# MLP second layer: half of the low weights of 11 chunks made by negation on ScalarE and an adding transfer instead of a subtraction on VectorE

## The chip, the cores and the metric

The kernel runs on one core of a Trainium2 chip. The metric is the device time of one execution in microseconds; lower is better. The kernel before takes 2065.62 us (median of two runs, 2065.62 and 2065.63).

## The reference, cut to what matters

One layer of an encoder over 256 tokens of width 2048, all float32: a mixer of two branches (retention and gated DeltaNet), cross-attention into 256 memory tokens, and an MLP, each behind an RMSNorm and with a residual sum; a last RMSNorm. The change touches the MLP's second matrix only:

```python
h = rms_norm(x, norm_ffn_g[l])
x = x + jnp.square(jax.nn.relu(h @ w_ff1[l])) @ w_ff2[l]   # w_ff1: 2048 x 8192, w_ff2: 8192 x 2048
return rms_norm(x, norm_final_g)
```

## The kernel before, in words

All large products run on TensorE in a type of reduced precision (float32r). To keep float32 accuracy each operand is split into a high and a low half: high = the value rounded to that type, low = value - high. A product is then three matmuls, high x high, high x low, low x high, summed in PSUM (lines 134 to 136 in `products`).

Weights stream from HBM. `fetch` (L75) takes one quarter of a chunk: 512 rows x 512 columns, 1 MB, loaded by one DMA on SP's queue into `raw` (3 buffers), seen as four row blocks of 128. For each of two halves (i = 0, 1; two row blocks, 128 x 1024 elements, 512 KB) ScalarE writes the high half `whi` (L93) and VectorE the low half `wlo` by subtracting `whi` from `raw` (L94). `whi` and `wlo` have 4 buffers each, so two quarters are held. A `raw` buffer is free once the last of its two subtractions is done. All this has a high priority, so it is put as early as buffers allow.

`chunk` (L120) multiplies 256 tokens by 512 columns of a weight matrix: four quarters q, each with 4 row blocks x 2 token blocks x 3 matmuls = 24 matmuls of 512 columns, 12 per half. The MLP is done in four groups (`fb`, L1066), each over 2048 hidden features: first eight `blocks` of w_ff1 (L158, the other form of product, lines 172 and 174), then three chunks (n = 1, 2, 3, L1093) of w_ff2. Columns 0 to 511 of w_ff2 are done another way, by Strassen's seven products (`seven_products`, L1014), one call per 512 hidden features; each call loads one `raw` of 1 MB and makes two halves of 21 matmuls of 256 columns (L1041 to L1043). In the first three groups two of the four calls fall among the w_ff1 blocks and two among the chunks.

The order on each engine is set by a scheduler from priorities and its own estimates when the program is built; then every engine works through its list in order and waits on semaphores. SP issues all the weight loads. POOL has only a few small operations: it computes reciprocal roots (L222, L608).

The last chunk of the program (fb = 3, n = 3) takes its weights for quarters 2 and 3 into other buffers (`hold`).

Of the kernel before, what the change touches and what calls it, by code (L numbers as in the profile page):

```python
# [10 lines left out]
F32 = mybir.dt.float32  # L11
F32R = mybir.dt.float32r
I32 = mybir.dt.int32
AF = mybir.ActivationFunctionType
ALU = mybir.AluOpType
# [35 lines left out]
def trunk(ctx: ExitStack, tc: tile.TileContext, x, mem, positions, norm_mix_g, w_in, conv_w, gdn_a_log, gdn_dt_bias,  # L51
# [4 lines left out]
    act, vec, pool, pe = nc.scalar, nc.vector, nc.gpsimd, nc.tensor  # L56
# [15 lines left out]
        return psp.tile([P, 512], F32, name="b", tag="b", bufs=4)  # L72


    def fetch(pieces, k, n, rush=False, hold=None, at=0):  # L75

        raw = wp.tile([P, k * n], F32, name="raw", tag="raw", bufs=3)
        rv = raw.rearrange("p (k n) -> p k n", k=k)
        with tc.high_priority(offset=100000):
            for off, ap in pieces:  # L80
                src = ap.rearrange("(k p) n -> p k n", p=P)
                for ks in ((slice(0, k // 2), slice(k // 2, k)) if rush else (slice(0, k),)):
                    nc.sync.dma_start(rv[:, ks, off:off + ap.shape[1]], src[:, ks, :])
            got = []
            for i in range(2):
                if hold:
                    both = hold().both
                    hi, lo = (both[:, a:a + 2, :].rearrange("p a s -> p (a s)") for a in (0, 2))
                else:
                    hi, lo = (wp.tile([P, 1024 + ROOM], F32R, name=e, tag=e, bufs=4)[:, at:at + k * n // 2]  # L90
                              for e in ("whi", "wlo"))
                src = raw[:, i * k * n // 2:(i + 1) * k * n // 2]
                act.activation(hi, src, AF.Copy)  # L93
                vec.tensor_sub(lo, src, hi.bitcast(F32))  # L94
                got.append((hi.rearrange("p (k n) -> p k n", n=n), lo.rearrange("p (k n) -> p k n", n=n)))
        return got

# [19 lines left out]
    def quad_a():  # L117
        return new_quad(hqp, 5)

    def chunk(quads, pieces_of, evac, before=None, hold=None, between=None):  # L120


        ps = stream_ps()
# [5 lines left out]
        def products(q, i, part, halves):  # L129
            t, c0, c1, o = part  # L130
            xh, xl = (a[:, i, t * P:(t + 1) * P] for a in quads[q])
            wh, wl = (a[:, i % 2, c0:c1] for a in halves[i // 2])
            first, last = q == 0 and i == 0, q == 3 and i == 3
            pe.matmul(o, xh, wh, start=first, stop=False)  # L134
            pe.matmul(o, xh, wl, start=False, stop=False)  # L135
            pe.matmul(o, xl, wh, start=False, stop=last)  # L136

        for q in range(4):
            if q not in held:
                if before:  # L140
                    before(q)
                halves = fetch(pieces_of(q), 4, 512, rush=before is not None and q == 0)
                for i in range(4):
                    for part in parts:
                        products(q, i, part, halves)
                    if between and i % 2:
                        between()
# [7 lines left out]
    def cols(w, c0, n=512):  # L155
        return lambda q: [(0, w[q * 512:(q + 1) * 512, c0:c0 + n])]
# [178 lines left out]
    for k2 in range(8):  # L335
# [10 lines left out]
        for f in range(2):  # L346
            k = 2 * k2 + f
# [203 lines left out]
    for q in range(4):  # L551
        at = slice(32 * q, 32 * q + 32)
# [513 lines left out]
    for fb in range(4):  # L1066
# [6 lines left out]
        for b2 in range(8):  # L1073
# [3 lines left out]
            at = slice(b2 % 2 * 2, b2 % 2 * 2 + 2)  # L1077
# [15 lines left out]
        for n in range(1, 4):  # L1093
# [13 lines left out]
            def evac_last(t, ps, c0, c1):  # L1107
# [20 lines left out]
                for c in (0, 3, 1, 2):  # L1128
# [14 lines left out]
            last = fb == 3 and n == 3  # L1143
            sums = []
            chunk(hid, cols(w_ff2[0, fb * D:(fb + 1) * D, :], n * 512), evac_last if last else evac_o,
                  hold=quad_b if last else None)
            if n < 3 and fb < 3:
                strassen(n + 1)
            if fb == 3 and n == 1:
# [34 lines left out]
```

## Time and profile before

| | before |
|---|---|
| median of the runs | 2065.62 us |
| the profiled execution | 2066.05 us |
| its span (first to last instruction) | 2064.3 us |
| granted TensorE clock | 0.999 |
| moved by DMA | 408.28 MB, mean 198 GB/s |
| L94, low halves on VectorE | 668 of 1223 ns |
| L93, high halves on ScalarE | 668 of 1060 ns |
| the 11 chunks and their Strassen calls | four stretches; the first about 1465 to 1536 us |

The profile shows one execution. A busy engine is one with an instruction running; matmuls overlap, so one of 390 ns starts every 0.227 us. A row of the order of time gives start, duration, engine, line and tile; brackets give the idle time of the engine before it and what ended it. A DMA row on SP is its issue; its landing is listed apart.

### The profile page before, as it was taken

The page shows a single profiled execution, that of the slowest core. Times are in us where ns is not written, and L with a number is a line of the kernel's source. Part 1 is how long each engine was busy: PE and PEld are TensorE (multiplying, and loading weights), DVE is VectorE, ACT ScalarE, POOL GpSimd, SP SyncE. Part 2 cuts the span into 40 slices and gives each one's busy share as a digit, 9 for nine tenths or more (in the row PEclk, how much of TensorE's full clock was granted, in tenths as well). Part 3 has the DMA queues.
Part 4 walks back from the last instruction along what each step waited for, and adds up shares of the span by engine and source line. Part 5 has one row for each costly group of instructions (what it writes and reads, how often), then busy time and mean ns, then how long its engine had stood idle before and what let it go on. Part 6 is the DMA issues. An engine that isn't in the chain of part 4 may idle for free.

```text
span 2064.3 us, 29089 instructions
## 1 busy us (share of the span) xinstructions
PE 2045.1 (99%) x11240; PEld 1774.0 (86%) x11240; DVE 1510.3 (73%) x2381; ACT 1132.2 (55%) x1669; POOL 26.9 (1%) x37
## 2 busy tenths in 40 slices
PE   8999999999999999999999999999999999999998
PEld 6888888888888888888888898888888888988887
DVE  6785888588957896688767665768758756775885
ACT  7564664556445644565456555555546545554664
POOL 0000000000000000000000000000000000000000
PEclk9999999999999999999999999999999999999999
DMA  8797655465556555655567664565656566656653
GB/s 302 229 313 233 207 192 199 164 208 181 198 183 199 183 195 189 189 182 180 189 192 234 194 193 147 182 189 181 224 184 198 179 204 194 194 194 195 192 198 129
DMA packets 328313, 408.28 MB, mean 198 GB/s; under 512 B 31200, under 2 KB 236528, under 8 KB 328048
## 3 DMA queue, kind: packets, MB, share of 16 engines
q1 hardware_dynamic: 328032, 405.92, 61.0%
q8 instruction: 88, 1.44, 0.3%
q10 hardware_dynamic: 144, 0.52, 0.1%
q14 instruction: 49, 0.40, 0.1%
HBM read 391.19 MB, written 15.22 MB: 197 GB/s over the span
## 4 chain that ended last, share of the span: by engine, by line
PE 97%; DMA 1%; SPq 1%; issue 0%; DVE 0%; ACT 0%; POOLq 0%; POOL 0%; DVEq 0%; ACTq 0%
PE s L172 34%; PE s L174 17%; PE s L135 12%; PE s L134 12%; PE s L136 12%; PE b L1041 1%; PE b L1042 1%; PE b L1043 1%; PE b L689 1%; DMA xc<-x 1%; PE b L590 1%; PE b L104 0%; PE b L105 0%; PE b L106 0%; SPq L290 0%
## 5 line engine op out<-in xcount | busy, mean ns | idle before, releaser
L94 DVE TENSOR_TENSOR wlo<-raw,whi 128x1024 fp32r<-128x1024 f32 x668 | 816.0, 1223 | 412.6 <-ACT whi L93 405.7
L93 ACT ACTIVATE whi<-raw 128x1024 fp32r<-128x1024 f32 x668 | 706.6, 1060 | 689.1 <-PE s L172 331.2
L172 PE MATMUL s<-q,whi 128*128 128x512 f32 x3072 | 959.7, 392 | 2.2 <-DVE bo L187 2.1
L174 PEld LDWEIGHTS s<-q,wlo 128*128 128x128 f32 x3072 | 575.3, 188 | 123.6
L174 PE MATMUL s<-q,wlo 128*128 128x256 f32 x3072 | 611.9, 280 | 0.0
L172 PEld LDWEIGHTS s<-q,whi 128*128 128x128 f32 x3072 | 468.8, 188 | 5.2 <-DVE bo L187 2.5
L134 PE MATMUL s<-whi,q 128*128 128x512 f32 x1136 | 443.6, 392 | 0.7 <-ACT whi L93 0.7
L135 PE MATMUL s<-wlo,q 128*128 128x512 f32 x1136 | 443.5, 390 | 0.6 <-DVE wlo L94 0.6
L136 PE MATMUL s<-whi,q 128*128 128x512 f32 x1136 | 441.8, 390 | 0.0
L135 PEld LDWEIGHTS s<-wlo,q 128*128 128x128 f32 x1136 | 213.9, 188 | 43.5 <-DVE wlo L94 1.1
L134 PEld LDWEIGHTS s<-whi,q 128*128 128x128 f32 x1136 | 213.7, 188 | 42.9 <-ACT whi L93 1.1
L136 PEld LDWEIGHTS s<-whi,q 128*128 128x128 f32 x1136 | 213.3, 188 | 42.8 <-DVE q L257 0.2
L541 DVE SCALAR_TENSOR_TENSOR acc<-bo,cw,acc 128x255 f32<-128x255 f32 (+1 forms) x144 | 61.3, 479 | 3.3 <-ACT acc L538 3.0
L1029 ACT ACTIVATE sh<-raw 128x768 fp32r<-128x768 f32 x32 | 27.1, 847 | 49.1 <-DMA raw<-w_ff 32.5
L187 DVE TENSOR_TENSOR bo<-bo,s 128x256 f32<-128x256 f32 x128 | 47.9, 415 | 0.0
L649 DVE TENSOR_TENSOR pr<-lw,tw 32x31 f32<-32x31 f32 (+15 forms) x124 | 40.2, 324 | 8.7 <-DMA lw<-scr_l 7.1
L651 DVE TENSOR_TENSOR tw<-tw,pr 32x31 f32<-32x31 f32 (+15 forms) x124 | 40.5, 327 | 2.2
L186 ACT ACTIVATE bo<-s 128x256 f32<-128x256 f32 x128 | 41.0, 370 | 0.0
L1030 DVE TENSOR_TENSOR sl<-tt,sh 128x1024 fp32r<-128x1024 f32 x32 | 39.1, 1223 | 0.0
L1029 ACT ACTIVATE sh<-tt 128x1024 fp32r<-128x1024 f32 x32 | 33.6, 1051 | 8.4 <-DVE tt L1023 8.4
L1043 PE MATMUL b<-sh,cm 128*128 128x256 f32 x128 | 35.5, 279 | 0.0
L1042 PE MATMUL b<-sl,cm 128*128 128x256 f32 x128 | 35.5, 279 | 0.0
(359 smaller groups left out, 1575.5 us busy)
## 6 DMA issues: line engine op xcount, KB each, us to landing
raw<-w_in SPq DMA_DIRECT2D x143, 1024.0 KB, 5.1
raw<-w_ff SPq DMA_DIRECT2D x128, 1024.0 KB, 5.8
raw<-w_xkv SPq DMA_DIRECT2D x31, 1024.0 KB, 6.4
raw<-w_out SPq DMA_DIRECT2D x16, 1024.0 KB, 5.9
raw<-w_xq SPq DMA_DIRECT2D x16, 1024.0 KB, 5.4
raw<-w_xo SPq DMA_DIRECT2D x16, 1024.0 KB, 5.4
dec_d<-dec_w SPq DMA_DIRECT2D x8, 384.0 KB, 7.9
dec<-dec_d SPq DMA_DIRECT2D x8, 384.0 KB, 4.2
```

The source lines that it names most:

```text
L93: act.activation(hi, src, AF.Copy)
L94: vec.tensor_sub(lo, src, hi.bitcast(F32))
L134: pe.matmul(o, xh, wh, start=first, stop=False)
L135: pe.matmul(o, xh, wl, start=False, stop=False)
L136: pe.matmul(o, xl, wh, start=False, stop=last)
L172: pe.matmul(ps[b], wh[:, b * P:(b + 1) * P], xhl, start=kk == 0, stop=False)
L174: pe.matmul(ps[b][:, :S], wl[:, b * P:(b + 1) * P], xh, start=False, stop=kk == KT - 1)
L187: vec.tensor_add(o, o, ps[b][:, :S])
L541: vec.scalar_tensor_tensor(acc[:, d:], ps[:, :S - d], cw[:, j, blk:blk + 1], acc[:, d:], op0=ALU.mult, op1=ALU.add)
L1029: act.activation(sh[:, xs, :], src, AF.Copy)
L1042: pe.matmul(o, lhs[0], sl[:, x, :], start=False, stop=False)
L1043: pe.matmul(o, lhs[1], sh[:, x, :], start=False, stop=last and i == 1 and (m % 2 == 1 or m == 6))
```

## The change

`fetch` gets a list `adding` of halves. For a half in it, ScalarE writes a second tile besides `whi`: `wlo` = -round(raw), by an activation with scale -1. Then POOL issues a DMA from `raw` to `wlo` with the operation add, SBUF to SBUF, 128 partitions x 4 KB, so that `wlo` = raw - round(raw). The subtraction on VectorE is left out for that half. `chunk` passes the list on, and the MLP's second layer gives (1,) for all its chunks but the last: 11 chunks x 4 quarters = 44 halves. The sum stands in `wlo` as float32 where the subtraction's result was rounded to float32r when it was written.

```diff
-    def fetch(pieces, k, n, rush=False, hold=None, at=0):
+    def fetch(pieces, k, n, rush=False, hold=None, at=0, adding=()):
...
                 act.activation(hi, src, AF.Copy)
-                vec.tensor_sub(lo, src, hi.bitcast(F32))
+                if i in adding:
+                    act.activation(lo, src, AF.Copy, scale=-1.0)
+                    pool.dma_start(lo.bitcast(F32), src, accum_op=ALU.add)
+                else:
+                    vec.tensor_sub(lo, src, hi.bitcast(F32))
...
-    def chunk(quads, pieces_of, evac, before=None, hold=None, between=None):
+    def chunk(quads, pieces_of, evac, before=None, hold=None, between=None, adding=()):
...
-                halves = fetch(pieces_of(q), 4, 512, rush=before is not None and q == 0)
+                halves = fetch(pieces_of(q), 4, 512, rush=before is not None and q == 0, adding=adding)
...
             chunk(hid, cols(w_ff2[0, fb * D:(fb + 1) * D, :], n * 512), evac_last if last else evac_o,
-                  hold=quad_b if last else None)
+                  hold=quad_b if last else None, adding=() if last else (1,))
```

Lines behind L93 have numbers 4 higher in the changed kernel (matmuls L138 to L140, subtraction L98; the negation is L95, the transfer L96).

ScalarE, the last two quarters of the third chunk of the first group, and the first loads for the next group. The number behind a name tells one buffer's use from another; a `whi` and the `raw` it is made from belong together. Before:

```order
L93 ACTIVATE whi_14394<-raw_14392 128x1024
L93 ACTIVATE whi_14398<-raw_14392 128x1024
L93 ACTIVATE whi_14428<-raw_14426 128x1024
L93 ACTIVATE whi_14432<-raw_14426 128x1024
L93 ACTIVATE whi_14468<-raw_14466 128x1024
```

The same place with the change:

```order
L93 ACTIVATE whi_14404<-raw_14402 128x1024
L95 ACTIVATE wlo_14409<-raw_14402 128x1024
L93 ACTIVATE whi_14408<-raw_14402 128x1024
L93 ACTIVATE whi_14439<-raw_14437 128x1024
L95 ACTIVATE wlo_14444<-raw_14437 128x1024
L93 ACTIVATE whi_14443<-raw_14437 128x1024
L93 ACTIVATE whi_14480<-raw_14478 128x1024
```

One negation per quarter has come in, ahead of the second high half.

ScalarE at the first chunk of the first group, with the change (before, the rows are the same without L95):

```order
L93 ACTIVATE whi_13926<-raw_13924 128x1024
L93 ACTIVATE whi_13930<-raw_13924 128x1024
L95 ACTIVATE wlo_13931<-raw_13924 128x1024
L93 ACTIVATE whi_13961<-raw_13959 128x1024
L93 ACTIVATE whi_13965<-raw_13959 128x1024
L183 ACTIVATE ho_13906<-s0_13820 128x256
L95 ACTIVATE wlo_13966<-raw_13959 128x1024
```

Here the negation stands behind the second high half; the second quarter's is also behind the evacuation of a w_ff1 block (L183).

TensorE, the first matmuls that read a half made by a transfer. Before:

```order
L134 MATMUL s0_13922<-whi_13930,q_13006 128x512
L135 MATMUL s0_13922<-wlo_13931,q_13006 128x512
L136 MATMUL s0_13922<-whi_13930,q_13006 128x512
L134 MATMUL s1_13923<-whi_13930,q_13006 128x512
L135 MATMUL s1_13923<-wlo_13931,q_13006 128x512
```

With the change:

```order
L138 MATMUL s0_13922<-whi_13930,q_13006 128x512
L138 MATMUL s1_13923<-whi_13930,q_13006 128x512
L139 MATMUL s0_13922<-wlo_13931,q_13006 128x512
L140 MATMUL s0_13922<-whi_13930,q_13006 128x512
L139 MATMUL s1_13923<-wlo_13931,q_13006 128x512
L140 MATMUL s1_13923<-whi_13930,q_13006 128x512
```

The second token block's high product has moved ahead of the first low product. Elsewhere in the groups some Strassen matmuls stand a few places earlier or later between the chunks' matmuls; all are there in the same number. SP's list of loads is the same in both.

POOL, from the last normalisation ahead of the MLP to the end, with the change:

```order
L226 TENSOR_TENSOR n_r<-n_s,nhalf_pow 128x2 x2
L96 DMA wlo<-raw 128x1024 x44
L226 TENSOR_TENSOR r_18909<-s_18906,nhalf_pow 128x1
L226 TENSOR_TENSOR r_18978<-s_18947,nhalf_pow 128x1
L1184 UNCONDITIONAL_BRANCH
```

The 44 transfers stand together, with nothing between them.

## The prediction

> **What bounds the kernel now.** I read the page from the span down, then TensorE's own waits, then the stretch where the change acts.
>
> ```profile
> span 2064.3 us, 29089 instructions
> PE 2045.1 (99%) x11240; PEld 1774.0 (86%) x11240; DVE 1510.3 (73%) x2381; ACT 1132.2 (55%) x1669; POOL 26.9 (1%) x37
> PE 97%; DMA 1%; SPq 1%; issue 0%; DVE 0%; ACT 0%; POOLq 0%; POOL 0%; DVEq 0%; ACTq 0%
> ...
> PE s L172 <- DVE bo L187: 2.1, 2, 1.1
> PE s L134 <- ACT whi L93: 0.7, 1, 0.7
> PE s L135 <- DVE wlo L94: 0.6, 1, 0.6
> ```
>
> TensorE is busy for all but 2064.3 - 2045.1 = 19.2 us, and the chain that ended last is its own matmuls to 97%. The last rows are the list of who waited for whom: matmuls waited for a low half (L94) once in the run, for 0.6 us. So a lighter VectorE has almost nothing to give back, and the question is whether the new way of making low halves stays ahead of TensorE.
>
> The stretch is the second layer of the MLP. The table by stretches gives, for its first group of three chunks (PE, PEld, DVE, ACT and POOL busy, clock, DMA share, GB/s):
>
> ```profile
> 1465.00:1536.00 71.00, 71.00 (x357) 60.41 (x356) 46.07 (x47) 32.48 (x32) 0.00 (x0) 1.00 0.60 196
> ```
>
> TensorE has no gap at all in these 71 us, at the full clock; VectorE is busy for 65%, ScalarE for 46%, POOL not at all, the DMA engines for 60%. What has room is read from the end of a chunk, in order of time (start, duration, engine, line; in brackets the idle time before and what ended it):
>
> ```profile
> 1513.54 1.06 ACT L93 ACTIVATE whi<-raw 128x1024 fp32r<-128x1024 f32 x1 [0.92 <-PE s L136]
> 1516.50 1.06 ACT L93 ACTIVATE whi<-raw 128x1024 fp32r<-128x1024 f32 x1 [1.90 <-PE s L136]
> 1521.42 1.06 ACT L93 ACTIVATE whi<-raw 128x1024 fp32r<-128x1024 f32 x1 [3.87 <-PE s L136]
> 1524.14 1.06 ACT L93 ACTIVATE whi<-raw 128x1024 fp32r<-128x1024 f32 x1 [1.66 <-PE s L136]
> 1526.86 1.06 ACT L93 ACTIVATE whi<-raw 128x1024 fp32r<-128x1024 f32 x1 [1.66 <-PE s L136]
> 1529.58 1.06 ACT L93 ACTIVATE whi<-raw 128x1024 fp32r<-128x1024 f32 x1 [1.66 <-PE s L136]
> 1532.30 1.06 ACT L93 ACTIVATE whi<-raw 128x1024 fp32r<-128x1024 f32 x1 [1.66 <-PE s L136]
> ...
> 1525.24 1.23 DVE L94 TENSOR_TENSOR wlo<-raw,whi 128x1024 fp32r<-128x1024 f32 x1 [1.49 <-ACT whi L93]
> ...
> 1526.49 0.37 SPq L83 DMA_DIRECT2D raw<-w_ff  x1
> ...
> 1537.54 1.06 ACT L93 ACTIVATE whi<-raw 128x1024 fp32r<-128x1024 f32 x1 [1.46 <-PE s L172]
> ```
>
> Each high half is made the moment TensorE lets go of one of the four buffers: one per 2.72 us, which is 12 matmuls. (Between 1516.50 and 1521.42 it is 4.92: one half of a Strassen block lies between, 2.2 us more.) The buffer filled at 1524.14 is read when three further halves are done, at the release that the row of 1532.30 shows; its low half is first read one matmul (0.23) later, about 1532.4. VectorE finishes it at 1525.24 + 1.23 = 1526.47. That is a cover of 5.9 us. The raw buffer is free at the same moment: its next load is issued at 1526.49, and its high half is wanted at 1537.54.
>
> **The change part by part.** In 11 chunks of four quarters, the second low half of each quarter is no longer VectorE's. ScalarE writes the negated high half, and a transfer issued by POOL adds the raw weights onto it.
>
> ```profile
> L94 DVE TENSOR_TENSOR wlo<-raw,whi 128x1024 fp32r<-128x1024 f32 x668 | 816.0, 1223 | 412.6 <-ACT whi L93 405.7
> L93 ACT ACTIVATE whi<-raw 128x1024 fp32r<-128x1024 f32 x668 | 706.6, 1060 | 689.1 <-PE s L172 331.2 <-PE s L136 277.0 <-DMA raw<-w_ff 39.5
> ```
>
> (1) Removed: 44 subtractions by 1.223 = 53.8 us of VectorE. It was not on the path; worth the 0.6 us of the wait above at most, taken as 0.
>
> (2) Added: 44 activations of the form of L93, 44 x 1.060 = 46.6 us of ScalarE, 4.2 us per chunk. In the 71 us stretch ScalarE goes from 32.5 to about 45 us; it lies in its waits for TensorE (1.66 us before each high half). Taken as 0; without that idle time each would shift the next high half by 1.06 us, against 5.9 of cover.
>
> (3) The new chain. The order puts the negation ahead of the second high half, so it starts at about 1524.14, as soon as the buffer is free, and ends at 1525.2. From there to 1532.4 there are 7.1 us (rounded down for the hand-over) for X: the wait of POOL, the issue, the transfer and its signal. Only at the first quarter of a group of chunks does the negation stand behind the second high half, and there 7.1 - 1.0 = 6.1 us are left. X has no row of its own. The nearest rows (issues: queue, count, size, median us from issue to landing; then an SP issue and an operation of POOL):
>
> ```profile
> raw<-w_ff SPq DMA_DIRECT2D x128, 1024.0 KB, 5.8
> vv_d<-vo SPq DMA_DIRECT2D x4, 512.0 KB, 4.7
> out<-res SPq DMA_DIRECT2D x1, 512.0 KB, 2.7
> xc<-x SPq DMA_DIRECT2D x4, 512.0 KB, 11.4
> ...
> L83 SPq DMA_DIRECT2D raw<-w_ff x7: 367/368/368, 1499.8 to 1531.9; - x7
> ...
> L608 POOL TENSOR_TENSOR nk<-ske,half_pow 128x4 f32<-128x4 f32 x8 | 8.1, 1007 | 456.5 <-DVE ske L599 266.7 <-DVE sc L605 189.8
> ```
>
> The transfer writes 512 KB but must read 1024 KB, raw and negated. Below, it is like 512 KB on idle engines: 0.37 + 2.7 = 3.1 us. Above, it is like 512 KB in the crowd of the start: 1.0 + 11.4 = 12.4. Between them I take the row with the same amount to read, under the same load: 5.8, with 1.0 for an issue that POOL makes (its longest operation), and 1.0 for sharing, because a weight load is in flight beside it (the share of 0.60 is loads). X = 7.8 us. The Trainium skill (DMA: Bandwidth & Descriptors, "Anatomy of one DMA") gives 2.0 us plus bytes over 436 GB/s for a POOL transfer, and Collectives: The Full Stack (Part 3, "Why ReduceScatter is half of AllGather" stands there) has an add read two sources; 1 MB would then be an estimated 4.4 us and no matmul would wait. The row of the 1 MB loads, 5.8, is longer than that estimate.
>
> An X over the cover makes TensorE wait for the excess e = X - 7.1 = 0.7 us. It does not wait at every quarter: the adding buffers are two of the four, and a wait for one gives the next the same time back, so at most one in two quarters waits, six per group of three chunks. Three of these six have Strassen halves (2.2 us each) inside their window and are covered up to e = 2.2. That leaves 3 + 3 + 3 + 2 = 11 waits over the four groups, and 1.0 more at the first of each group: 11 x 0.7 + 4 x 1.0 = 11.7 us.
>
> (4) Behind it, the raw buffer is now let go at the end of the transfer: 1525.2 + 7.8 = 1533.0, 6.5 us later than 1526.49. SP's queue stands in order behind that load, the Strassen raws too. The load lands 5.8 later at 1538.8 (one more with sharing) where 1537.54 was wanted; the 1.3 to 2.3 us come out of ScalarE's idle time of 1.7 and then out of the 5.9 us of the first half. The ring of three raws turns in 5.8 + 1.0 + 2.1 + 7.8 = 16.7 us where three quarters take 16.3; the 0.13 us per quarter are less than the Strassen blocks give (4.4 us each, two per group). Taken as 0.
>
> (5) POOL's queue: nothing else stands between its transfers (the order ahead of this shows it), and its next operation, the last normalisation, comes after them. TensorE's matmuls are the same ones; some are put ahead of the first that needs a transferred half (two L134 together), worth 0.2 us each, within the rounding.
>
> The sum: the profiled execution took 2066.05 us, 1.75 around its span; 2066.05 + 11.7 = 2077.75; the median of the runs is 0.43 below that execution. Forecast: 2077.3 us.
>
> **The rivals.** *The cover holds.* If X is at most 6.1, no matmul waits: 2065.6 us, or up to 0.6 less. For it: 512 KB rows of 2.7 and 4.7. Against: those copies read only 512 KB.
>
> *The DMA engines run out.* In the stretch, 0.60 x 71 = 42.6 us of engine time move 196 x 71 = 13.9 MB, 3.2 us per load of 1.05 MB. Charged by what it reads, an accumulation also takes 3.2. A group has 14 loads and 12 accumulations in it, 83.2 us, where TensorE needs 12 x 5.44 + 4 x 2.2 = 74.1. That is 9.1 late per group, over 11/3 groups 33 us: 2099. Against: charged by what it writes, it is 64 us, and fits.
>
> *Slower by over 2%: POOL gets to write its transfers late.* All the excess would come at one place, between the end of the negation and the first packet. VectorE runs in rows without a gap:
>
> ```profile
> 1471.18 1.22 DVE L94 TENSOR_TENSOR wlo<-raw,whi 128x1024 fp32r<-128x1024 f32 x1
> 1472.32 1.22 DVE L1011 TENSOR_TENSOR cm<-cb,cm 128x1024 fp32r<-128x1024 f32 x1
> 1473.45 0.68 DVE L1023 TENSOR_TENSOR tt<-tt,raw 128x512 f32<-128x512 f32 x1
> 1474.05 1.22 DVE L94 TENSOR_TENSOR wlo<-raw,whi 128x1024 fp32r<-128x1024 f32 x1
> ```
>
> If POOL cannot write while VectorE runs, it waits for the end of such a row, 4 us here, some 2.5 on average. X is then 10.3 and e 3.2; now the other six-less-three waits count too, with e - 2.2: (11/3) x (3 x 3.2 + 1.0 + 3 x 1.0) = 50 us, 2116. It passes 2% (41 us) from e = 2.8, X about 9.9. At the upper bound, X = 12.4, e is 5.3 and it is (11/3) x (15.9 + 1.0 + 9.3) = 96 us: 2162. For it: VectorE is 65% busy here, and POOL has issued no transfer in this trace. Against: its small operations show one steady time (1007 ns, eight times). The Trainium skill (SBUF — State Buffer, "SBUF: two separate sides") warns of just this for POOL's transfers under VectorE's two-port modes, with 620 ns becoming 3100; it also says that an operation with two SBUF inputs blocks only POOL work that reads SBUF, so by that sentence L94 would not count. No run so far shows which.
>
> *Faster.* All of TensorE's idle time is 19.2 us, most of it at the ends; over 2% (41 us) cannot come from waits.
>
> **How the numbers follow.** The forecast (2068 to 2090) gets 0.42; the cover that holds 0.25; the DMA engines running out (2090 to 2107) 0.13; late POOL transfers (over 2107) 0.19; faster by over 2% 0.01. About 2% is what a measurement here can tell from no change. So faster 0.01, within 2% 0.42 + 0.25 + 0.13 = 0.80, slower 0.19. The range runs from the cover that holds, 2064.5, to the edge of the late transfers with the nearer part of them, 2112; the forecast's own range is 2068 to 2090.
>
> **What would show it.** Right: waits of PE L135 (now L139) for the added transfer on a low half, about 10 to 15 of some 0.5 to 2 us, mostly in the first chunk and at the end of the third of each group; VectorE's subtractions down by 44; SP's loads of w_ff2 issued about 6 us later; X near 8 us. Wrong at step 3: no such waits, or an X beyond 9.9 with a wait at every second quarter. Wrong at step 4: ScalarE waiting for raw weights for over 2 us at a time, and a DMA share near 1. The clock should stay at 1.00; if it moves, my sum leaves out its cause.

## The result, and the profile after

The changed kernel takes 2138.33 us (median of two runs, 2137.85 and 2138.81) where the kernel before takes 2065.62: a ratio of 1.0352, 95% interval 1.0307 to 1.0396, or 72.7 us more. The forecast was 2077.3, with 2112 as the upper end of the range.

The page of the changed kernel: the span, the busy time of each engine, the shares of the chain that ended last, then that chain's lines; last, the granted clock.

```profile
span 2137.1 us, 29280 instructions
PE 2068.3 (97%) x11240; PEld 1780.0 (83%) x11240; DVE 1460.1 (68%) x2337; ACT 1168.7 (55%) x1713; POOL 64.9 (3%) x81
PE 79%; DMA 14%; issue 4%; ACT 1%; DVE 1%; SPq 1%; POOLq 0%; POOL 0%; ACTq 0%; DVEq 0%
PE s L176 31%; PE s L178 16%; PE s L139 9%; PE s L140 9%; PE s L138 9%; DMA wlo<-raw 8%; DMA raw<-w_ff 5%; PE b L693 1%; ACT wlo L95 1%; DMA xc<-x 1%; PE b L594 1%; PE b L108 0%; PE b L109 0%; PE b L110 0%; SPq L294 0%
```

```profile
core 0: 2137.1 us, clock 0.992
```

TensorE is idle for 2137.1 - 2068.3 = 68.8 us, 49.6 more than before. It is also busy for 2068.3 - 2045.1 = 23.2 us more with the same 11240 matmuls. Of these 23.2 about 14.6 are the granted clock, by an estimate (2068.3 x (1/0.992 - 1/0.999); the other of the two runs had 0.987). I put the rest down to matmuls that start after a gap: in the chain of waits the first one behind a gap counts 0.50 us, at 1534.40 and at 1547.93, and those that follow count 0.23. No run isolates this part. The chain, 97% TensorE before, now has 14% of DMA in it: the adding transfers (8%) and the loads of w_ff1 and w_ff2 (5%). VectorE gave up 44 subtractions for nothing.

Who waited for whom (us in total, times, the longest):

```profile
ACT whi L93 <- DMA raw<-w_ff: 132.3, 41, 9.0
ACT sh L1033 <- DMA raw<-w_ff: 61.2, 15, 6.9
PE s L139 <- DMA wlo<-raw: 36.4, 23, 2.9
PE b L1045 <- ACT sh L1033: 9.5, 8, 3.0
SPq L83 <- DMA wlo<-raw: 271.1, 37, 11.7
```

TensorE's own new waits are mostly for low halves made by a transfer, 36.4 us in 23. But ScalarE's row comes earlier in the chain: it waited 132.3 us for raw weights, up to 9.0 at a time, where the row quoted in the prediction has 39.5. And SP's queue waited 37 times for a transfer to end before it could issue the next load. The negation, and with it the transfer, starts late because the raw weights are late; they are late because an earlier transfer still held their buffer.

The first group of chunks (PE, PEld, DVE, ACT and POOL busy, clock, DMA share, GB/s), and in order of time the chain of waits in it (start, duration, what):

```profile
1450.00:1550.00 100.00, 87.84 (x430) 72.24 (x429) 38.88 (x43) 48.16 (x52) 10.47 (x12) 0.98 0.80 217
```

```profile
1476.65 4.51 DMA wlo<-raw
1481.30 5.83 DMA raw<-w_ff
...
1489.54 10.00 DMA wlo<-raw
1499.55 5.48 DMA raw<-w_ff
1505.16 0.71 issue
1505.87 1.05 ACT wlo L95
1506.92 0.34 issue
1507.26 9.06 DMA wlo<-raw
1516.47 4.94 DMA raw<-w_ff
1521.72 0.75 issue
1522.47 1.05 ACT wlo L95
1523.53 0.34 issue
1523.87 10.49 DMA wlo<-raw
```

Load, negation, transfer, load: nothing of TensorE is in this ring, and the ring sets the pace. (The load at 1499.55 is a Strassen call's. The negation at 1505.87 reads other weights; it stands behind the Strassen call's first high half in ScalarE's list and waits with it.) One turn takes 1523.87 - 1507.26 = 16.6 us, and the prediction has 16.7. The agreement is partly luck. In the rows of that turn the load lands in 4.9, where the prediction has 6.8 (5.8 and 1.0 for sharing), and the transfer with its start takes 9.4, where it has 7.8. The transfers also differ from each other: the one at 1476.65 took 4.5 us, with no load issued while it ran, and the three at 1489.54, 1507.26 and 1523.87, each with a load issued within 0.3 us of it, took 9.1 to 10.5. TensorE, without a gap here before, now stands still for 12.2 of 100 us, and the DMA share has gone from 0.60 to 0.80.

What the new operations cost (one transfer's issue with its count, busy time and mean ns; the negation; the median us from issue to landing; packets, MB and share of the DMA engines for POOL's queue):

```profile
L96 POOL DMA_DIRECT2D wlo<-raw x44 | 38.0, 864 | 688.5 <-ACT wlo L95 666.2
L95 ACT ACTIVATE wlo<-raw 128x1024 fp32r<-128x1024 f32 x44 | 46.0, 1046 | 1.4 <-PE s L139 1.4
wlo<-raw POOLq DMA_DIRECT2D x44, 512.0 KB, 7.4
q0 software_dynamic: 6336, 23.07, 5.6%
```

From negation to landed half it is 0.34 (the "issue" rows above) + 7.4 = 7.7 us in the median: the X of the prediction was 7.8. The 44 transfers took 5.6% of all DMA engines' time, 0.056 x 2137.1 / 44 = 2.7 us each.

### The profile page after: what moved, and what is told of

Its sections match the earlier page's. It is cut to its first block, busy times and chain, and to the rows that moved or that the text cites. A ratio compares the mean times of both kernels' runs of the same rounds, so it can differ in the third digit from the quotient of the medians.

```text
span 2137.1 us, 29280 instructions
## 1 busy us (share of the span) xinstructions
PE 2068.3 (97%) x11240; PEld 1780.0 (83%) x11240; DVE 1460.1 (68%) x2337; ACT 1168.7 (55%) x1713; POOL 64.9 (3%) x81
## 3 DMA queue, kind: packets, MB, share of 16 engines
q0 software_dynamic: 6336, 23.07, 5.6%
## 4 chain that ended last, share of the span: by engine, by line
PE 79%; DMA 14%; issue 4%; ACT 1%; DVE 1%; SPq 1%; POOLq 0%; POOL 0%; ACTq 0%; DVEq 0%
PE s L176 31%; PE s L178 16%; PE s L139 9%; PE s L140 9%; PE s L138 9%; DMA wlo<-raw 8%; DMA raw<-w_ff 5%; PE b L693 1%; ACT wlo L95 1%; DMA xc<-x 1%; PE b L594 1%; PE b L108 0%; PE b L109 0%; PE b L110 0%; SPq L294 0%
## 5 line engine op out<-in xcount | busy, mean ns | idle before, releaser
L93 ACT ACTIVATE whi<-raw 128x1024 fp32r<-128x1024 f32 x668 | 704.9, 1059 | 695.3 <-PE s L176 323.0
L98 DVE TENSOR_TENSOR wlo<-raw,whi 128x1024 fp32r<-128x1024 f32 x624 | 761.6, 1222 | 464.7 <-ACT whi L93 457.8
L139 PE MATMUL s<-wlo,q 128*128 128x512 f32 x1136 | 451.5, 397 | 39.5 <-DMA wlo<-raw 36.4
L138 PE MATMUL s<-whi,q 128*128 128x512 f32 x1136 | 444.9, 396 | 2.4 <-ACT whi L93 2.4
L140 PE MATMUL s<-whi,q 128*128 128x512 f32 x1136 | 446.7, 394 | 0.0
L138 PEld LDWEIGHTS s<-whi,q 128*128 128x128 f32 x1136 | 216.0, 190 | 46.2 <-ACT whi L93 3.0
L140 PEld LDWEIGHTS s<-whi,q 128*128 128x128 f32 x1136 | 216.4, 191 | 43.2
L1033 ACT ACTIVATE sh<-raw 128x768 fp32r<-128x768 f32 x32 | 26.9, 842 | 67.2 <-DMA raw<-w_ff 61.2
L96 POOL DMA_DIRECT2D wlo<-raw x44 | 38.0, 864 | 688.5 <-ACT wlo L95 666.2
L1025 DVE TENSOR_TENSOR tt<-raw 128x1024 f32<-128x1024 f32 x16 | 19.6, 1224 | 56.4 <-DMA raw<-w_ff 56.4
L95 ACT ACTIVATE wlo<-raw 128x1024 fp32r<-128x1024 f32 x44 | 46.0, 1046 | 1.4 <-PE s L139 1.4
L1033 ACT ACTIVATE sh<-tt 128x1024 fp32r<-128x1024 f32 x32 | 33.7, 1054 | 15.3 <-DVE tt L1027 15.3
```

The source lines that it names most:

```text
L95: act.activation(lo, src, AF.Copy, scale=-1.0)
L1033: act.activation(sh[:, xs, :], src, AF.Copy)
```

## The experiments

The expectations name theories by letter. Two are left at the end: A, that the raw buffers let go later are the cause, and C, that it is the DMA engines' time that the transfers take. D, in the runs between, stands for both at once. Times of the kernel before in the same rounds lay at 2064.9 to 2065.3 us, and losses below are against those. The edits shown are cut to the lines that matter. Eleven runs need room for another tile: the last norm then loads 512 or 1024 of its 2048 gains and uses 512 of them for all columns. One of these runs, own raw buffer with 22 transfers, lost 7 us in all, so this edit by itself can't be what makes losses of 30 to 80.

**The other half by transfer.** The raw buffer is let go when both the transfer, under way since the first half, and the second half's subtraction are done.

```diff
-                  hold=quad_b if last else None, adding=() if last else (1,))
+                  hold=quad_b if last else None, adding=() if last else (0,))
```

> One number changed: the first half of each quarter is made by the transfer and the second by the subtraction. Theory A (the raw buffers are let go late, and the ring of three that the Strassen loads share starves): the transfer starts one half (2.72 us) earlier in the quarter, so raw is free that much earlier; the chain transfer, next load, high half, negation, transfer shrinks from about 17.5 to 15 us and half or more of the loss goes: 2075 to 2100 us. Rival B (the low half itself comes too late for its own cover, the four low buffers): the cover of a first half is the same as that of a second, so 2130 to 2145 us. Rival C (transfers and loads slow each other on the DMA engines): same bytes, 2130 to 2145 us.

2127.24 us, ratio 1.028 (1.0241 to 1.0319). Only some 11 us back, where A wanted 2075 to 2100 and the rivals 2130 to 2145: a miss for all three. The four runs lie between 2113.65 and 2131.67, so the 11 are rough. In the same stretch the loads of weights still took 7.3 us to land instead of 5.5.

**A raw buffer of its own for Strassen.**

```diff
-        raw = wp.tile([P, 2048], F32, name="raw", tag="raw", bufs=3)
+        raw = fp.tile([P, 2048], F32, name="raws", tag="raws", bufs=1)
```

> The changed kernel with a raw buffer of its own for the Strassen loads, so that the three are the chunks' alone; to make room for it the last normalisation uses the first 512 gains for all four quarters of the columns, and loads 256 KB of them and not 1 MB. Theory A: the ring of three then turns in 5.8 + 2.1 + 8.5 = about 16.4 us per three quarters of 16.3, and most of the loss goes: 2075 to 2100 us. Rival B: the covers of the low halves are as before, 2125 to 2140. Rival C: same bytes, 2125 to 2140.

2098.39 us, 1.0163 (1.0148 to 1.0178): over half of the loss is gone. Its waits:

```profile
PE s L139 <- DMA wlo<-raw: 9.7, 10, 1.6
ACT whi L93 <- DMA raw<-w_ff: 32.0, 15, 6.0
```

With three buffers for quarters alone, step 3 of the prediction comes out: 10 waits for transferred halves, 9.7 us in all, where 11 and 11.7 were forecast. That points at the ring. But 33 us remain. Some of it may come from the new buffer, of which there is only one: ScalarE now waits 85.2 us for the Strassen weights, where it waited 61.2 with the change.

**The traffic without the hold.** All low halves by subtraction again; beside them the same 44 adds, from a tile that nobody waits for onto tiles that nobody reads, started when the subtraction is done.

```diff
+                vec.tensor_sub(lo, src, hi.bitcast(F32))
                 if i in adding:
-                    act.activation(lo, src, AF.Copy, scale=-1.0)
-                    pool.dma_start(lo.bitcast(F32), src, accum_op=ALU.add)
-                else:
-                    vec.tensor_sub(lo, src, hi.bitcast(F32))
+                    to, still = spare()
+                    pool.tensor_copy(to[:, 0:1], lo[:, 0:1].bitcast(F32))
+                    pool.dma_start(to, still[:, 0:1024], accum_op=ALU.add)
```

> The low halves are all made by the subtraction as before the change; POOL issues 44 adding transfers at the same places (after a one-column copy that waits for the second low half), but from a tile that stays still (the gains) onto two tiles that nothing reads. The last normalisation uses the first 512 gains for all quarters. No raw and no low half waits for a transfer; what is left is traffic. Theories A and B: no loss, 2064 to 2072 us. Rival C: most of the loss, 2110 to 2140 us.

2107.07 us, 1.0202 (1.0182 to 1.0222): 42 us from traffic that nothing depends on (the trace lists no wait of VectorE for POOL's copy or for an add). A alone cannot be all. The time from issue to landing of the chunk and w_ff1 loads between 1465 and 1545 us (least, median, most), for the kernel before:

```profile
DMA to landing us min/median/max: 4.9/5.5/5.8
```

For this one:

```profile
DMA to landing us min/median/max: 5.2/11.9/13.4
```

And for the change itself:

```profile
DMA to landing us min/median/max: 4.9/9.0/10.0
```

The page of the change gives 5.9 for all 128 loads, and 5.8 before, because most of them run beside no transfer. Only the stretch shows more: 9.0 (4.9 at best), and 11.9 beside the free adds. These medians are thin, since the trace tells the landing of 6 of 14, 4 of 12 and 4 of 10 loads there. And in the change the loads on the chain shown above are the quick ones, 5.8, 5.5 and 4.9 us: what the two streams cost each other fell on the transfers there, that is on the hold.

**The same with the raw weights as source**, so that the raw buffer is held as well.

```diff
-                    pool.dma_start(to, still[:, 0:1024], accum_op=ALU.add)
+                    pool.dma_start(to, src, accum_op=ALU.add)
```

> As the kernel with the still source, but the 44 transfers read raw, so each raw buffer is let go only when its transfer is done, as in the changed kernel; the low halves come from the subtraction and no matmul waits for a transfer. The last normalisation uses the first 512 gains for all quarters. Theory A: nearly all of the loss, 2115 to 2140 us. Rival B: no loss, 2064 to 2075 us. Rival C: the same as with the still source, within 10 us.

2130.64 us, 1.0316 (1.0295 to 1.0337): 65 us, some 24 on top of the traffic. The three loads of this stretch whose landing is told took 4.9, 5.3 and 6.8 us, not far from the 4.9 to 5.8 before, so here it is the late buffer and not a slow load that shows. This is nearly the whole loss, with no matmul reading a transferred half: that low halves come late for TensorE is a consequence at most.

**The negation alone**, with the subtraction kept and no transfer.

```diff
                     act.activation(lo, src, AF.Copy, scale=-1.0)
-                    pool.dma_start(lo.bitcast(F32), src, accum_op=ALU.add)
-                else:
-                    vec.tensor_sub(lo, src, hi.bitcast(F32))
+                vec.tensor_sub(lo, src, hi.bitcast(F32))
```

> ScalarE's 44 negations alone: they are written into the low tile, then the subtraction overwrites them; no transfers. All theories: the 46.6 us of ScalarE lie in its idle time, 2064 to 2070 us. If ScalarE's queue were part of the cause: over 2075 us.

2065.21 us, 0.9999 (0.9988 to 1.0011): nothing. (One of its eight runs took 11773 us and is left out of the ratio; nothing in the runs says why.)

**Plain copies instead of adds**, in the changed kernel, and **plain copies from the still tile** in the run with traffic alone.

```diff
-                    pool.dma_start(lo.bitcast(F32), src, accum_op=ALU.add)
+                    pool.dma_start(lo.bitcast(F32), src)
```

> The changed kernel with the transfers as plain copies instead of adds (the low halves are then the raw weights, so the product is another one); issue, queue, waits and bytes written are the same. Theory D (after the first runs: the adds take the DMA engines' time, 2.7 us of all 16 per transfer by their packets, and the raw buffers are held for it): a copy needs about half, 1.3 us, the landing falls from 7.4 to 4 to 5 us, and over half of the loss of 73 us goes: 2070 to 2100 us. Rival E (POOL's issue of 0.9 us and the fixed part of any transfer, with the buffers held behind it): 2110 to 2135 us.

> As the kernel with the still source (2107 us), but plain copies instead of adds; all else the same, the last normalisation again with the first 512 gains for all quarters. Theory D: the engines need 1.3 us and not 2.7 per transfer, so the 42 us fall to 0 to 12: 2065 to 2078 us. Rival E (44 POOL transfers of this size as such, or the one-column copy on POOL): 2095 to 2110 us.

2097.06 us, 1.0154 (1.0125 to 1.0184), and 2081.93, 1.008 (1.0034 to 1.0126): 32 and 17 us, where the adds cost 73 and 42. The row of POOL's queue on the page of the first of them, and its transfers' median landing:

```profile
q0 software_dynamic: 6336, 23.07, 2.7%
wlo<-raw POOLq DMA_DIRECT2D x44, 512.0 KB, 6.1
```

The same packets and bytes take 2.7% of the engines' time instead of 5.6%: a copy of 512 KB is 1.3 us on all engines, an add 2.7. Halving the engine time more than halves the loss. The hold is left in, but it is shorter too: the copies land in 6.1 us where the adds take 7.4. For the still tile the expectation was at most 2078, and the three runs spread from 2076 to 2088.

**Three buffers more for the transferred halves.**

```diff
+                if i in adding:
+                    lo = spare.tile([P, 1024], F32R, name="wadd", tag="wadd", bufs=3)
```

> The changed kernel with three buffers of their own for the halves that the transfers make (they share four with the others otherwise), so that each may come 5.4 us later without a wait; the last normalisation uses the first 512 gains for all quarters. Theory D: raw buffers and DMA engines are the limit, so most of the loss stays: 2115 to 2140 us, with the waits moved from the transfers to the high halves. Rival B (the low half's own cover): 2066 to 2095 us.

2115.51 us, 1.0244 (1.0214 to 1.0273). The negation can start earlier, and TensorE's waits for transfers vanish from the list; 23 us come back. The other 50 are lost all the same, in waits behind raw weights:

```profile
ACT wadd L97 <- DMA raw<-w_ff: 95.6, 23, 7.8
PE b L1047 <- ACT sh L1035: 31.4, 8, 6.5
```

**Every second quarter only**, 22 transfers.

```diff
-                halves = fetch(pieces_of(q), 4, 512, rush=before is not None and q == 0, adding=adding)
+                halves = fetch(pieces_of(q), 4, 512, rush=before is not None and q == 0, adding=adding if q % 2 == 0 else ())
```

> The changed kernel with transfers in quarters 0 and 2 of each chunk only, 22 instead of 44. Theory D (DMA engines and raw buffers run out): the engines then need 2 x 3.1 + 2.7 = 8.9 us per two quarters of 10.9, where they need 11.6 with 44, so the loss falls by much more than half: 2066 to 2088 us. Rival F (every transfer costs its own share): half of 73, about 2102 us, 2096 to 2108.

2065.43 us, 1.0002 (0.9993 to 1.0012). Half the transfers cost nothing, not half. The stretch:

```profile
1450.00:1550.00 100.00, 100.00 (x524) 85.91 (x524) 56.30 (x61) 51.38 (x58) 5.32 (x6) 1.00 0.76 232
```

TensorE has no gap; the DMA engines move more (232 GB/s) at a lower share (0.76). So there is no price per transfer. There is a limit that 44 pass and 22 don't.

**Each add in the still-tile kernel as two of half the row length** (2 KB instead of 4 KB per partition).

```diff
-                    pool.dma_start(to, still[:, 0:1024], accum_op=ALU.add)
+                    for a in (0, 512):
+                        pool.dma_start(to[:, a:a + 512], still[:, a:a + 512], accum_op=ALU.add)
```

> As the kernel with the still source (2107 us), but each add is cut into two transfers of 2 KB per partition. Theory G (the engines take turns by packet, so that a load's packet of 2 KB in 0.095 us waits for an add's of 4 KB in 0.328): the loads get more of the engines while adds are under way, 2078 to 2098 us. Rival H (only the total of engine time counts): 2100 to 2114 us.

2097.79 us, 1.0159 (1.0138 to 1.0179): 9 us less than with long rows, at the upper end of what was expected if packets take turns. But the edit does more than shorten rows: the second of each pair waited for the first (95.7 us in 43 waits of POOL), and VectorE waited for POOL four times, up to 8.8 us. What the row length does by itself isn't shown.

**First half and own raw buffer together; own raw buffer with 22 transfers.** The edits are those above, two at a time.

> A raw buffer for the Strassen loads (2098 us by itself) and the first half of each quarter by the transfer (2127 by itself); the last normalisation uses the first 512 gains for all quarters. Theory D: both let raw buffers come back earlier, and a fourth buffer leaves less to gain: 2080 to 2096 us. If the place of the add in the quarter does not matter once the buffers are four: 2096 to 2101 us.

> A raw buffer for the Strassen loads and only 22 transfers; the last normalisation uses the first 512 gains for all quarters. Theory D: the engines and the buffers both have room, so the loss is gone to a few us: 2064 to 2074 us. If a transfer costs TensorE something by itself even then: 2080 us or more.

2107.66 us, 1.0206 (1.0186 to 1.0227), 9 us worse than the own buffer with the second half: a miss, and its cause stays open. 2072.58 us, 1.0036 (1.002 to 1.0051): as expected, but 7 us worse than 22 transfers in the shared ring. So a Strassen buffer of its own, of which there is one, has a price; no run has it without transfers and without a hold.

**The hold with next to no traffic.** Instead of one add, three small ones (64 bytes per partition) from the raw weights, each waiting for the one before.

```diff
+                    for _ in range(3):
+                        pool.dma_start(to[:, 0:16], src[:, 0:16], accum_op=ALU.add)
```

> The low halves all by the subtraction; after the second of each quarter POOL issues three adds one after the other, each of 64 bytes per partition from raw onto a tile that nothing reads, so that raw is let go some 7 us later with almost no bytes moved; the last normalisation uses the first 512 gains for all quarters. Theory I (late raw buffers cost by themselves): the step between the still source and the raw source, 23 us, or more: 2080 to 2100 us. Theory J (they cost only because loads are slowed by the adds' engine time): 2064 to 2074 us.

2143.66 us, 1.0382 (1.0352 to 1.0412): 79 us, more than the change and more than either side expected. It looks like proof of A. But 24 of the 44 chains began on POOL right behind the one before, without a wait for a subtraction: POOL set part of the pace there, and the size says little.

**Adds of half the width**, the rest of those low halves by subtraction.

```diff
-                if i in adding:
-                    act.activation(lo, src, AF.Copy, scale=-1.0)
-                    pool.dma_start(lo.bitcast(F32), src, accum_op=ALU.add)
-                else:
-                    vec.tensor_sub(lo, src, hi.bitcast(F32))
+                m = 512 if i in adding else 0
+                if m:
+                    act.activation(lo[:, :m], src[:, :m], AF.Copy, scale=-1.0)
+                    pool.dma_start(lo[:, :m].bitcast(F32), src[:, :m], accum_op=ALU.add)
+                vec.tensor_sub(lo[:, m:], src[:, m:], hi[:, m:].bitcast(F32))
```

> The changed kernel with 44 adds of half the width (512 of 1024 elements per partition); VectorE subtracts for the other 512. Engine time is 1.35 us per transfer, in all as for the 22 whole ones that cost nothing. If engine time decides: 2064 to 2074 us. If the number of transfers and the hold of raw in every quarter decide, as with the plain copies (2097 us): 2085 to 2105 us.

2100.04 us, 1.0171 (1.0141 to 1.02). These 44 take 3.2% of the engines' time, hardly more than the 2.9% of the 22 long ones that cost nothing; yet 35 us are lost. Engine time alone isn't the limit either: here every quarter's raw buffer is held, there every second.

**The hold tied to TensorE.** All low halves by subtraction; POOL copies one column of the raw weights into a low tile that the matmuls have done with, after the quarter's first half, after its second, and after its second with an own buffer for Strassen. The line for the second (the first has i == 1):

```diff
+                    if adding and i == 3:
+                        pool.tensor_copy(halves[i // 2][1][:, 1, 0:1], halves[2][:, 0:1])
```

> All low halves by subtraction, no transfer, no negation. In the 11 chunks POOL copies one column of each quarter's raw weights into the first half's low tile once the matmuls have read it (nothing reads it again), so the raw buffer is let go when TensorE has done the quarter's first half. By the profile of the kernel before that is about 5.9 us after the last subtraction (1526.47 to 1532.4), near the 6 to 8 us of the adding transfer, and with next to no bytes moved; POOL is in no chain of its own as it was with three small transfers. If late raw buffers in the ring of three shared with the Strassen loads are the cause (theory A), 2085 to 2115 us and ScalarE's waits for raw weights as long as with the change. If the transfers' engine time has to be there too (theory C), at most 2072.

> As the run that lets go after the quarter's first half, but after its second: 2.7 us later, 8.6 us behind the last subtraction, a little longer than the adding transfer holds it. Theory A: 2100 to 2150 us. Theory C: at most 2075.

> As the run that lets go after the quarter's second half, with the Strassen weights in a raw buffer of their own (the final norm's gains are cut to 512 columns and used over and over for that, so the output is scaled by other gains). The ring then serves quarters alone: 5.8 + 1.0 + 2.1 + 8.6 = 17.5 us a turn where three quarters take 16.3. Theory A in the form that the Strassen raw makes two buffers of three: at least half of that run's loss comes back, 2066 to 2095 us. If the ring is too short even for quarters alone, it stays within 10 us of that run.

2070.63 us, 1.0025 (1.0016 to 1.0034); 2074.62, 1.0048 (1.0031 to 1.0065); 2071.83, 1.0029 (1.0018 to 1.0041). A is far off: 5.5 and 9.5 us, and the own buffer wins back at most 3 of them. This hold was long, 7.1 us in the rows below (VectorE's subtractions end at 1514.09 + 2.36, SP's load is issued at 1523.52), yet TensorE had no gap in the stretch. It has a way out, though: when weights run short, TensorE reads a half as soon as it is there, and the buffer is let go at once. Eight holds of this group, matched by their order, go from 4.3 to 9.1 us, so this hold isn't fixed. That the way out is what makes it cheap is argued; no run tests it alone. The rows, in order of time (VectorE, POOL, SP; then the stretch):

```profile
1514.09 2.36 DVE L94 TENSOR_TENSOR wlo<-raw,whi 128x1024 fp32r<-128x1024 f32 x2 [1.13 <-ACT whi L93]
...
1522.57 0.93 POOL L149 CAST wlo<-raw 128x1 fp32r<-128x1 f32 x1 [7.21 <-PE s L137]
...
1523.52 0.37 SPq L83 DMA_DIRECT2D raw<-w_ff  x1
...
1450.00:1550.00 100.00, 100.00 (x522) 85.73 (x522) 63.53 (x67) 45.49 (x51) 6.65 (x12) 1.00 0.59 200
```

**A fixed hold that POOL keeps up with**: two small adds in place of three.

```diff
-                    for _ in range(3):
+                    for _ in range(2):
```

> As the run with three chained small transfers from the raw weights, but two (128 partitions x 64 bytes each; low halves by subtraction; the final norm's gains cut to 512 columns and used over and over, so the output is scaled by other gains). With three, POOL was busy or waiting for about 8 us per quarter where TensorE takes 5.44, so POOL's own chain set the pace; with two it is about 0.5 + 0.4 + 0.9 + 1.5 + 0.9 = 4.2 us and POOL keeps up. The raw buffer is then held some 5 to 6 us behind the subtraction, by a fixed time and not until TensorE has read the half (which let the hold shrink whenever TensorE ran short of weights). If a late buffer alone costs what the change cost (theory A), the loss is at least half of the change's: over 2100 us. If the later release costs little as long as the DMA engines have room (theory C, and what the two runs tied to TensorE showed with 5.5 and 9.5 us), 2068 to 2080 us.

2111.42 us, 1.0221 (1.0205 to 1.0236): 46 us, A's side of the expectation. The rows of a quarter, from the end of its last subtraction to the next load into its buffer:

```profile
1491.86 2.36 DVE L94 TENSOR_TENSOR wlo<-raw,whi 128x1024 fp32r<-128x1024 f32 x2 [2.22 <-ACT whi L93]
...
1494.29 0.18 POOL L97 COPY side<-wlo 128x1 f32<-128x1 f32 x1 [2.13 <-DVE wlo L94]
1494.84 0.85 POOL L99 DMA_DIRECT2D side<-raw  x1 [0.36 <-POOL side L97]
1499.61 0.87 POOL L99 DMA_DIRECT2D side<-raw  x1 [3.92 <-DMA side<-raw]
...
1501.86 0.37 SPq L1025 DMA_DIRECT2D raw<-w_ff  x1
```

The stretch, with the columns as above, and the landing of its loads:

```profile
1450.00:1550.00 100.00, 94.59 (x477) 79.06 (x476) 56.26 (x59) 39.90 (x44) 24.49 (x36) 1.00 0.60 178
```

```profile
DMA to landing us min/median/max: 5.0/5.2/6.2
```

The hold is 1501.86 - 1494.22 = 7.6 us (longer than I planned, since the small add of 1494.84 landed after 4.4 us, at 1499.3). Over the run it isn't as fixed as its name: matched by order, the holds go from 5.2 to 13.5 us, 8.4 in the mean. POOL waited for the subtraction in 32 of 44 quarters; in the other 12 it was late, matched in the same way, by at most some 3.5 us and by 14 in sum, so it is seldom the bound. The DMA share is that of the kernel before, and loads land in 5.2 us. A buffer that comes late by a time TensorE can't shorten, with free DMA engines, costs some 46 us.

**What the runs say together.** Two things that the change does each cost over half of the loss when they stand alone: the hold (46 us) and the transfers' traffic (42). Together they cost 65 to 73, not 88. My account is that both draw on one reserve: the turns that three raw buffers can make. A sum in buffer time tests it. A group of three chunks has 3 x 74.1 = 222 us of buffer time (74.1 is TensorE's time from the prediction). A Strassen raw stays far longer than a quarter's. The kernel before, SP's two loads and the last reading of the first:

```profile
1486.01 0.37 SPq L1020 DMA_DIRECT2D raw<-w_ff  x1
...
1511.70 0.96 DVE L1030 TENSOR_TENSOR sl<-raw,sh 128x768 fp32r<-128x768 f32 x1 [1.03 <-ACT sh L1029]
...
1512.68 0.37 SPq L83 DMA_DIRECT2D raw<-w_ff  x1
```

That is 26.7 us, and a group has two, 53. With 12 quarters of landing + 2.1 (two activations) + what then holds it (the last subtraction's end 1.3, or 0.3 and the transfer), the estimates are:

| | a quarter's buffer | 12 quarters and Strassen, of 222 us | late, over 11/3 groups | TensorE idle, more than before | loss |
|---|---|---|---|---|---|
| before | 5.5 + 2.1 + 1.3 = 8.9 | 160 | 0 | 0 | 0 |
| 22 transfers | 8.9 and 5.4 + 2.1 + 0.3 + 5.4 = 13.2 | 186 | 0 | -1 | 0 |
| traffic alone | 11.9 + 2.1 + 1.3 = 15.3 | 237 | 18 | 23 | 42 |
| fixed hold alone | 5.2 + 2.1 + 1.3 + 7.6 = 16.2 | 247 | 31 | 24 | 46 |
| the change | 9.0 + 2.1 + 0.3 + 7.0 = 18.4 | 274 | 63 | 50 | 73 |
| plain copies | 5.9 + 2.1 + 0.3 + 6.0 = 14.3 | 225 | 3 | 19 | 32 |
| adds of half the width | 5.8 + 2.1 + 0.3 + 4.5 = 12.7 | 205 | 0 | 21 | 35 |
| hold tied to TensorE | 5.6 + 2.1 + 1.3 + 7.1 = 16.1 | 246 | 29 | 2 | 9.5 |

(5.4, 7.0, 6.0 and 4.5 are the medians of transfers in the stretch. Late is the excess over 222 divided by three buffers. It is to be set against TensorE's idle time on the pages, since the rest of a loss is time in which TensorE is busy longer with the same matmuls.) For the first five rows the order and the threshold come out; the last three don't. The hold tied to TensorE comes out only with its own Strassen raws, which stayed 16.2 and 15.1 us in that group (224, and 3 late): the stay is itself an outcome and can't be taken over from the kernel before. For plain copies and half-width adds the sum sees nothing of some 20 us. One thing that it leaves out shows in the half-width run: SP works through its list in order, so the buffer that the Strassen weights left at 1489.45 got its next load at 1493.20 only, behind a load that waited for a transfer. Whether that is all is open. So the sum is an estimate: late buffers are shown as a cause by the runs that isolate them, and the size isn't modelled. How the 73 us divide between hold and traffic can't be said, since they don't add.

No version here beats the kernel before. TensorE was busy for all but 19.2 us of it, and the best, 22 transfers, equals it.

## Why the prediction was wrong

- **Steps 1, 2 and 5 held.** 44 subtractions fewer brought nothing, the negations cost nothing (2065.21 us alone), POOL issued at once.
- **Step 3 held in its price, in the median and with some luck.** X was 7.7 us for 7.8, between bounds of 3.1 and 12.4. But it isn't one size: on the chain shown a transfer took 4.5 us with no load issued while it ran, and 9.1 to 10.5 with one. By the Trainium skill's formula (DMA: Bandwidth & Descriptors, "Anatomy of one DMA") the prediction estimated 4.4 us for the DMA. The least of the 44 took 4.5, so the trace agrees for a transfer without a load beside it and not for the others: the median is 7.4. The waits, 36.4 us in 23 instead of 11.7 in 11, came from raw weights that were late, not from X: with raw weights less late, in the own-buffer run, they were 9.7 in 10.
- **Step 4 failed: "The ring of three raws turns in 5.8 + 1.0 + 2.1 + 7.8 = 16.7 us where three quarters take 16.3; the 0.13 us per quarter are less than the Strassen blocks give (4.4 us each, two per group). Taken as 0."** The turn's length was met (16.6 in the chain), with a load that was shorter and a transfer that was longer than the terms. Wrong was to let three quarters share the buffers and to take the rest as 0: the Strassen loads pass through the same three buffers and each stays long (26.7 us in the rows of the kernel before), in which quarters have two. I counted the time that a Strassen block gives TensorE and left out the buffer that it takes. In the term's place the runs showed 46 us for a hold alone (7.6 us in the rows shown, 8.4 in the mean), and 40 of the 73 us back when the Strassen loads got a buffer of their own.
- **The DMA engines, a rival at 2099 with 0.13, were a cause too.** Their traffic alone cost 42 us. The priced term was near: 2.7 us of engine time per add (3.2 taken), 3.2 + 2.7 = 5.9 per quarter against 5.44. Its form was not. I set it beside the ring as a case of its own, where it lengthens the ring's turn: beside a load a transfer took 9.1 to 10.5 us, and that is the time for which the raw buffer is held. The two belonged into one sum.
- **Late POOL transfers (0.19, over 2107)** gave a time of that size for a reason that isn't there: 44 issues took 0.84 to 1.05 us each. VectorE was at work during 26 of them, and none of these took over 0.89. That agrees with the sentence of the Trainium skill (SBUF — State Buffer, "SBUF: two separate sides") by which an operation with two SBUF inputs blocks only POOL work that reads SBUF.
- **The clock moved** from 0.999 to 0.992, about 15 us that the sum left out, as it said. The run with 22 transfers, without gaps, stayed at 1.00 in the stretch.
- Of the signs named for a failure of step 4 one was seen in full, ScalarE waiting up to 9.0 us for raw weights, and one in part: the DMA share rose to 0.80, where a share near 1 was named.

## What to carry to other kernels

A transfer that reads a streamed buffer holds it until the transfer has landed: SP's next loads waited for that 37 times here. Before moving work there, add up the buffer time of everything that passes through the ring (landing under the new traffic, processing, hold), other users with long stays included, and set it against buffers x time. A sum above that is a warning; a sum below it is no promise: here plain copies lost 32 us with a sum at the limit, and half-width adds 35 with one well below. Take a transfer's landing time from the stretch in which it runs beside others, not from the page's median; and check that an experiment which isolates a hold isn't bound by the engine that makes it.

## What the runs showed of the hardware

- An adding transfer takes twice the engine time of a plain copy of the same bytes: 5.6% against 2.7% of the span's DMA time for the same 6336 packets and 23.07 MB.
- Small transfers don't land fast beside large ones: 64 bytes per partition took 2.3 us in the median of the run with three, but up to 7.7; the one of 1494.84 above, 4.4.
- TensorE's gaps cost more than their length: 49.6 us more idle time came with 23.2 us more busy time for the same matmuls, and the mean clock of the run fell to 0.992 (0.98 in the stretch with the gaps). The clock doesn't go by the length of the gaps alone: in the same 100 us the free adds left 7.1 us of gaps at a clock of 0.95, the fixed hold 5.4 at 1.00.
